# An untied rotary product and a re-searched order in a two-layer attention trunk

## The chip, the cores and the metric

One core of a Trainium2 chip runs the whole program. The metric is the device time of one execution in microseconds. Every time below comes from the runs of the kernel before or from one profiled execution of it.

## The reference

The program computes a decoder trunk of two layers on one sequence of 256 tokens of width 1024. Each layer projects the normalised stream, runs attention with 16 heads of 64, gates it, projects it back, and adds a gated per-layer embedding. Layer 0 is block attention (with 256 tokens it is plain causal attention within one block), layer 1 has a compressed, a selected-block and a windowed branch. What the change touches is the norm and rotation of queries and keys:

```python
def rms_norm(x, gain):
    y = xf * lax.rsqrt(jnp.mean(xf * xf, axis=-1, keepdims=True) + NORM_EPS)
    return (y * gain)
def rope(x, pos):
    ...
    x1, x2 = xf[..., :half], xf[..., half:]
    return jnp.concatenate([x1 * cos - x2 * sin, x2 * cos + x1 * sin], axis=-1)
def moba_layer(h, w_in, q_gain, k_gain, w_out, pos):
    q, k, v, z = jnp.split(h @ w_in, 4, axis=-1)
    q = rope(rms_norm(split_heads(q, N_HEADS), q_gain), pos)
    k = rope(rms_norm(split_heads(k, N_HEADS), k_gain), pos)
    v = split_heads(v, N_HEADS)
    o = merge_heads(moba_attention(q, k, v)) * jax.nn.silu(z)
    return o @ w_out
def reference(...):
    for i in range(DEPTH):
        h = rms_norm(x, norm_gain[i])
        x = x + (moba_layer if i % 2 == 0 else nsa_layer)(h, ...)
        gate = jax.nn.sigmoid(rms_norm(x, ple_gate_gain[i]) @ ple_w_gate[i])
        x = x + gate * (p[i] @ ple_w_proj[i])
```

## The kernel before

**The work.** All weights pass through the core once, in tiles of 128x1024 f32 (512 KB) that SyncE's queue loads into five `raw` buffers. A float32 product is made of reduced-precision parts: ScalarE copies a tile to its rounded part `hi`, VectorE subtracts to get `lo` (`lo<-raw,hi`), and TensorE runs three products (high by high, high by low, low by high) into PSUM banks `mm`. Activations are split in the same way (`a`, `hl`). Scores go into banks `s`, are masked and scaled by VectorE (`sm<-s,...,nr_q`, which also gives the row's extreme in `nb`), exponentiated by ScalarE, divided by their sums `l` (`sm<-sm,l`, on VectorE or ScalarE), and transposed by TensorE (`tr<-cst,sm`).

**The rotation.** `rope()` takes 512 columns of queries or keys, 8 heads of 64, for two halves of 128 tokens. ScalarE squares them, VectorE sums the squares per head (`ssq`) and makes `r0` by two small `tensor_scalar`s, GpSimd raises `r0` to the power -1/2 (`r_q`, `r_k`), and for queries VectorE negates that into `nr_q`, which scales the scores. The rotation itself is two products with a sine table (`turn(t, 0)` and `turn(t, 1)`: `tmp<-q,tq`), one product with a cosine table (`q<-q,tq`) and a sum (`q<-q,tmp`) for each half; `finish()` issues what does not stand ahead of the power. In most rotations the factors are read from the bank of the matmul (`mm`). For the second eight heads of layer 0 (steps `1q` and `1k` of the order) the steps `1qe` and `1ke` have ScalarE copy the bank into the tile `q` or `k` first (`rope_evac`), so that both factors of each product lie in SBUF.

**The order.** Nothing is issued as it is written. Each operation is recorded, and `Plan.schedule`, a greedy list scheduler with a table of costs, places them on the engines; all are then emitted from one line, L400 of the profile. Ties go to what was recorded first, so the sequence of step names in the string `PROGRAM` sets the priorities. Names there are units of projections (`1q.2`), loads (`w:...`), head pairs (`S` scores, `T` transposes, `V` values), evacuations, and so on; names that begin with `n` or a group number are layer 1's. `nc.together(since)` glues the operations recorded since then into one run on their engine, with nothing between them: in `rope()` these are the two `r0` operations and `turn(0, 0)`. The profile names tiles by what the buffer is called first: `r` stands for `r0`, `hl` for the split pair of queries and keys of a head pair, `tq` and `tk` for the tables. Some evacuations may go to either ScalarE or VectorE, by what the scheduler finds free.

**The end.** The last stage is the gate of layer 1: eight units of matmuls (`ng0a` to `ng1b`), each evacuated by a chain (ScalarE copies half a bank, VectorE adds the other half and multiplies by `bc`, ScalarE takes a tanh, VectorE multiplies by the embedding and adds to `xT`), and the output is stored.

Of the kernel before, what the change touches and what calls it, by code (L numbers as in the profile page):

```python
# [24 lines left out]

PROGRAM = ("x0 w:c0 c0 x1 w:c1 c1 x2 w:c2 x3 w:c3 x4 w:c4 w:k.0 x5 c2 w:c5 c3 x7 consts tq a.1 x6 a.3 a.5 a.6 w:c6 a.7 w:c7 "
# [24 lines left out]

STORES = 5

# [368 lines left out]
def trunk(ctx: ExitStack, tc: tile.TileContext, a, out):  # L422
# [14 lines left out]
    def tmp(name):  # L437
        return work.tile([P, 512], F32, tag="tmp", name=name, bufs=5)
# [37 lines left out]
    def tables(name, gain, gains):  # L476
        t = work.tile([P, 2, 2, len(gains), HD], F32, tag=name[:2] + str(len(gains)), name=name, bufs=1)
        for b, g in enumerate(gains):
            for i, c in enumerate((cos, sin)):
                nc.vector.tensor_tensor(t[:, i, :, b], c, gain[:, g, i][:, None].to_broadcast([P, 2, HD]), op=OP.mult)  # L480
        return t
# [186 lines left out]
        return o  # L668

    def rope(ps, tab, nb, norm, is_q, tag, bufs, o=None):  # L670
        if o is None:
            o = work.tile([P, 2, 512], F32, tag=tag, name=tag, bufs=bufs)
        else:
            ps = [o[:, t] for t in range(2)]
        o = o.rearrange("p t (h d) -> p t h d", d=HD)
        ssq = work.tile([P, 2, 8], F32, tag="ssq", name="ssq")
        for t in range(2):
            sq = tmp("hsq").rearrange("p (h d) -> p h d", d=HD)
            nc.scalar.activation(sq.rearrange("p h d -> p (h d)"), ps[t], AF.Square)
            nc.vector.tensor_reduce(ssq[:, t], sq, axis=AX.X, op=OP.add)  # L680
        r0 = work.tile([P, 2, 8], F32, tag="r0", name="r0")
        g = 8 // nb
        qss = [tmp("qs").rearrange("p (b g d) -> p b g d", b=nb, d=HD) for _ in range(2)]
        vs = [ps[t].rearrange("p (b g d) -> p b g d", b=nb, d=HD) for t in range(2)]

        def tb(i, t, lo, hi):
            return tab[:, i, t, :, None, lo:hi].to_broadcast([P, nb, g, hi - lo])

        def turn(t, c):
            lo, hi = 32 * c, 32 * c + 32  # L690
            nc.vector.tensor_tensor(qss[t][:, :, :, lo:hi], vs[t][:, :, :, 32 - lo:64 - lo], tb(1, t, lo, hi), op=OP.mult)

        since = len(nc.ops)
        for t in range(2):
            nc.vector.tensor_scalar(r0[:, t], ssq[:, t], 1.0 if is_q else 1.0 / HD,
                                    norm.e2[:, 0 if is_q else 1, t:t + 1], op0=OP.mult, op1=OP.add)

        turn(0, 0)
        nc.together(since)
        r = work.tile([P, 2, 8], F32, tag="r_" + tag, name="r_" + tag, bufs=bufs)  # L700
        nc.gpsimd.tensor_tensor(r.rearrange("p t h -> p (t h)"), r0.rearrange("p t h -> p (t h)"), neg_half, op=OP.pow)
        if is_q:
            nr = work.tile([P, 2, 8], F32, tag="nr_" + tag, name="nr_" + tag, bufs=bufs)
            nc.vector.tensor_scalar(nr, r, -1.0, None, op0=OP.mult)
        def finish():
            for t in range(2):
                ot = o[:, t].rearrange("p (b g) d -> p b g d", b=nb)
                if t:
                    turn(t, 0)
                turn(t, 1)  # L710
                nc.vector.tensor_tensor(ot, vs[t], tb(0, t, 0, HD), op=OP.mult)
                nc.vector.tensor_tensor(ot, ot, qss[t], op=OP.add)
                if not is_q:
                    nc.vector.tensor_tensor(o[:, t], o[:, t], r[:, t, :, None].to_broadcast([P, 8, HD]), op=OP.mult)

        return o, (nr if is_q else None), finish
# [227 lines left out]
    class Half:  # L944
# [17 lines left out]
        def q(self):  # L962
            self.Q, self.nr, self.q2 = rope(self.u["q"].ps, tab["q"], 1, n0, True, "q", 2, self.early.get("q"))

        def k(self):
            self.K, _, self.k2 = rope(self.u["k"].ps, tab["k"], 1, n0, False, "k", 2, self.early.get("k"))
# [126 lines left out]
    def tabs2():  # L1093
# [4 lines left out]
                ntk=lambda: tab1.update(k=tables("tk1", gnsa, [2, 3])))  # L1098
# [163 lines left out]
    def rope_k():  # L1262
        ST["kk"], _, todo["KE+"] = rope(units["ks"].ps, tab1["k"], 2, n2, False, "q", 2)
# [55 lines left out]
    def KD(i):  # L1319
        w = ST["wins"][:, 960 * i:960 * i + 960].rearrange("p (t g n) -> p t g n", t=16, g=4)  # L1320
        cg = ST["cc"][i].rearrange("p (g t) -> p g t", g=4)
        for h in range(2):
            src = cg[:, :, 16 * h:16 * h + 240].rearrange("p g (n t u) -> p t g n u", t=8, u=2)[:, :, :, :, 0]
            nc.vector.tensor_tensor(w[:, 8 * h:8 * h + 8], src,
                                    pe[:, i, 8 * h:8 * h + 8, None, None].to_broadcast([P, 8, 4, 15]), op=OP.add)
        ST["win"][i] = w.rearrange("p t g n -> p t (g n)")
# [77 lines left out]
    for g in range(4):  # L1404
# [3 lines left out]
                KD0=lambda: KD(0), KD1=lambda: KD(1))  # L1408
# [134 lines left out]
```

## Time and profile before

| | us |
|---|---|
| median of 3 runs | 359.84 |
| lowest and highest run | 358.97, 360.23 |
| profiled execution, its own time | 358.39 |
| its span in the profile | 356.6 |
| TensorE busy in it | 349.5 (98%) |
| VectorE busy | 333.1 (93%) |
| ScalarE busy | 277.1 (78%) |
| GpSimd busy | 32.9 (9%) |

The profiled execution is 1.45 us (0.4%) shorter than the median of the runs and shorter than each of them; 1.79 us of its time lie outside the span. Its mean granted clock of TensorE is 0.998. The shares are averages over the span: what bounds a stage is read from the windows of that stage and from what each engine waited for there.

### The profile page before, as it was taken

To read this page: it belongs to the slowest core of one execution; us is meant where nothing else is said; L and a number is where in the kernel's file an instruction comes from. 1 tells how busy PE (TensorE), PEld (TensorE's weight loads), DVE (VectorE), ACT (ScalarE), POOL (GpSimd) and SP (SyncE) were. 2 spreads that over 40 slices of the span, in tenths; PEclk is the share of its full clock that TensorE was granted. 3 is DMA by queue.
4 is the path that set the end of the run, shared out by engine and by line. 5 is a ranking of instruction groups with operands and counts; after the bars stand their busy time and mean duration, and the time that the engine had idled before them with its cause. 6 is when DMAs were issued, how large, how long until landed. Compare 5 with 4: busy or idle time off the path is not lost.

```text
span 356.6 us, 6708 instructions
## 1 busy us (share of the span) xinstructions
PE 349.5 (98%) x2311; PEld 307.1 (86%) x2311; DVE 333.1 (93%) x846; ACT 277.1 (78%) x622; POOL 32.9 (9%) x26
## 2 busy tenths in 40 slices
PE   8999999989999999999999999999999999999995
PEld 7888888867999888888889999877998998888884
DVE  5899999979999999989999999999999999899875
ACT  5785699957999946768674899988989999857532
POOL 1044200432000000000003300003020000000000
PEclk9999999999999999999999999999999999999999
DMA  8989562711715367474636754427672331266012
GB/s 270 354 325 278 210 227 78 249 59 37 259 63 176 96 205 237 125 234 144 207 99 190 211 172 153 139 84 287 219 239 90 119 120 59 65 199 211 0 47 74
DMA packets 20770, 58.95 MB, mean 165 GB/s; under 512 B 2560, under 2 KB 6016, under 8 KB 20736
## 3 DMA queue, kind: packets, MB, share of 16 engines
q1 hardware_dynamic: 20160, 58.04, 50.2%
q10 hardware_dynamic: 576, 0.48, 0.4%
q8 instruction: 18, 0.29, 0.4%
q14 instruction: 16, 0.13, 0.1%
HBM read 57.46 MB, written 1.05 MB: 164 GB/s over the span
## 4 chain that ended last, share of the span: by engine, by line
PE 95%; DVE 2%; POOL 2%; ACT 0%; issue 0%; DVEq 0%; ACTq 0%
PE mm L400 75%; PE tr L400 13%; PE s L400 6%; POOL r_q L400 2%; DVE lo L400 1%; DVE sm L400 0%; DVE q L400 0%; DVE ssq L400 0%; DVE tmp L400 0%; DVE hl L400 0%; ACT hl L400 0%; DVE r L400 0%; ACT tmp L400 0%; DVE xT L400 0%; DVEq L1538 0%
## 5 line engine op out<-in xcount | busy, mean ns | idle before, releaser
L400 PE MATMUL mm<-a,hi 128*128 128x256 f32 (+1 forms) x656 | 153.1, 327 | 0.0
L400 ACT ACTIVATE hi<-raw 128x1024 fp32r<-128x1024 f32 (+2 forms) x100 | 99.8, 1008 | 37.3 <-PE mm L400 21.3
L400 DVE TENSOR_TENSOR lo<-raw,hi 128x1024 fp32r<-128x1024 f32 (+2 forms) x100 | 115.5, 1164 | 6.5 <-ACT hi L400 5.7
L400 PE MATMUL mm<-hi,a 128*128 128x512 f32 (+2 forms) x356 | 103.9, 378 | 0.0
L400 PEld LDWEIGHTS mm<-a,hi 128*128 128x128 f32 x656 | 101.7, 190 | 1.8 <-DVE big L400 0.2
L400 PE MATMUL mm<-a,lo 128*128 128x256 f32 x448 | 103.0, 283 | 0.0
L400 PEld LDWEIGHTS mm<-a,lo 128*128 128x128 f32 x448 | 81.9, 189 | 9.6 <-issue 0.2
L400 PEld LDWEIGHTS mm<-hi,a 128*128 128x128 f32 x356 | 64.6, 192 | 10.4 <-DVE hi L400 0.2
L400 PE MATMUL mm<-lo,a 128*128 128x512 f32 (+2 forms) x178 | 64.1, 375 | 0.0
L400 ACT ACTIVATE sm<-sm,nb 128x128 f32<-128x128 f32 (+1 forms) x96 | 42.8, 451 | 2.5 <-DVE nb L400 2.3
L400 PEld LDWEIGHTS mm<-lo,a 128*128 128x128 f32 x178 | 33.6, 192 | 5.1
L400 DVE CUSTOM_DVE_ANT_0 sm<-s,cst,nr_q 128x256 f32<-128x256 f32 (+1 forms) x80 | 31.7, 428 | 0.3
L400 POOL TENSOR_TENSOR r_q<-r,neg_half 128x16 f32<-128x16 f32 x5 | 18.0, 3593 | 80.9 <-DVE r L400 80.9
L400 ACT ACTIVATE pt<-tr 128x384 f32<-128x384 f32 x48 | 22.3, 489 | 2.1 <-PE tr L400 1.8
L400 PE MATMUL tr<-cst,sm 128*128 128x128 f32 x144 | 23.1, 274 | 0.0
L400 ACT ACTIVATE tmp<-tmp 128x256 f32<-128x256 f32 (+3 forms) x26 | 12.1, 471 | 10.4 <-DVE tmp L400 10.4
L400 PEld LDWEIGHTS tr<-cst,sm 128*128 128x128 f32 x144 | 17.3, 141 | 3.3 <-ACT sm L400 0.8
L400 ACT ACTIVATION_READ_ACCUMULATOR sm<-sm,nb 128x1 f32 x96 | 18.6, 194 | 0.0
L400 POOL TENSOR_TENSOR rstd<-ms,neg_half 128x2 f32<-128x2 f32 x4 | 3.0, 741 | 169.2 <-DVE ms L400 169.2
L400 ACT ACTIVATE a<-xT,gain_in 128x256 fp32r<-128x256 f32 x31 | 14.6, 498 | 4.8 <-DVE xT L400 2.1
L400 DVE TENSOR_TENSOR hl<-tr,hl 64x512 fp32r<-64x512 f32 x24 | 16.5, 689 | 1.2 <-ACT hl L400 0.4
L400 PE MATMUL tr<-pt,v 128*64 128x256 f32 (+1 forms) x192 | 17.1, 330 | 0.0
(170 smaller groups left out, 452.2 us busy)
## 6 DMA issues: line engine op xcount, KB each, us to landing
raw<-in_moba_in SPq DMA_DIRECT2D x28, 512.0 KB, 4.5
raw<-in_nsa_in SPq DMA_DIRECT2D x24, 512.0 KB, 4.2
raw<-in_w_o SPq DMA_DIRECT2D x8, 512.0 KB, 3.7
raw<-in_w_g SPq DMA_DIRECT2D x8, 512.0 KB, 4.3
raw<-in_w SPq DMA_DIRECT2D x8, 512.0 KB, 4.0
raw<-in_w_no SPq DMA_DIRECT2D x8, 512.0 KB, 3.6
raw<-in_w_ng SPq DMA_DIRECT2D x8, 512.0 KB, 4.1
raw<-in_ple_proj SPq DMA_DIRECT2D x4, 512.0 KB, 4.8
```

The lines of the kernel that those rows point to most:

```text
L400: getattr(getattr(self.nc, o.engine), o.method)(*[real(x) for x in o.args], **{k: real(x) for k, x in o.kwargs.items()})
```

## The change

Two things. First, in `rope()` the product `turn(0, 0)` is recorded ahead of the power, and glued behind the `r0` operations, only where the factors are read from the matmul's bank. For copied queries and keys it is recorded in `finish()`, free to be placed anywhere. Second, the string `PROGRAM` is another one from the masks of layer 0 on, through both layers to the end. The scheduler, its costs, the buffers and all sizes are the same.

```diff
@@ PROGRAM (about 30 lines of it, of which the first changed one)
-           "w:1q.0 w:1q.3 1q.0 masks w:1k.0 consts1 A0 w:1q.1 w:1k.2 w:1k.3 A2 S2 w:1q.2 S0 v A3 1q.1 S3 w:1v.0 w:1v.1 "
...
+           "w:1q.0 w:1q.3 1q.0 masks w:1k.0 A0 w:1v.0 w:1q.1 A3 w:1v.1 w:1q.2 w:1v.2 S3 1q.1 1q.2 1q.3 w:1k.2 S0 A2 1k.0 1qe "
...
@@ rope()
-        if o is None:
+        in_bank = o is None
+        if in_bank:
             o = work.tile([P, 2, 512], F32, tag=tag, name=tag, bufs=bufs)
...
-        turn(0, 0)
+        if in_bank:
+            turn(0, 0)
         nc.together(since)
...
         def finish():
             for t in range(2):
...
-                if t:
+                if t or not in_bank:
                     turn(t, 0)
                 turn(t, 1)
```

What the two do to VectorE's queue at the copied queries' rotation, between the two `r_0<-ssq` operations and the `hl` operations that follow. Names are the buffers' (`q_139` the copied queries, `tq_0_129` their tables, `s_154` and `s_155` score banks, `r_q_145` GpSimd's power, `tr_75` a bank of transposed queries and keys). VectorE before:

```order
L400 TENSOR_SCALAR r_0_142<-ssq_140,e_0_135 128x8 x2
L400 TENSOR_TENSOR tmp_82<-q_139,tq_0_129 128x8x32
L400 TENSOR_TENSOR tmp_83<-q_139,tq_0_129 128x8x32
L400 TENSOR_TENSOR tmp_82<-q_139,tq_0_129 128x8x32
L400 TENSOR_TENSOR tmp_83<-q_139,tq_0_129 128x8x32
L400 TENSOR_TENSOR lo_123<-raw_126,hi_115 128x1024
L400 TENSOR_TENSOR q_139<-q_139,tq_0_129 128x512 x2
L400 TENSOR_SCALAR nr_q_147<-r_q_145 128x16
L400 TENSOR_TENSOR q_139<-q_139,tmp_82 128x512
L400 TENSOR_TENSOR q_139<-q_139,tmp_83 128x512
L400 TENSOR_TENSOR hl_150<-tr_75,hl_150 64x512 x2
```

Behind the two `r_0` stand seven operations on two SBUF tiles each, then `nr_q`, the sums and `hl`. VectorE after, the same place, in two pieces:

```order
L400 TENSOR_SCALAR r_0_142<-ssq_140,e_0_135 128x8 x2
L400 ISA sm_68,nb_156<-s_154,tmp_85,nr_q_146 128x128
L400 ISA nb_156 128x1
L400 TENSOR_TENSOR tmp_86<-s_155,cst_65 128x128
L400 TENSOR_SCALAR sm_71<-sm_71,l_153 128x128
L400 TENSOR_SCALAR sm_71<-sm_71,l_153 128x256
L400 TENSOR_SCALAR sm_72<-sm_72,l_153 128x128
L400 TENSOR_SCALAR sm_72<-sm_72,l_153 128x256
L400 TENSOR_TENSOR tmp_83<-q_139,tq_0_129 128x8x32
L400 TENSOR_TENSOR tmp_84<-q_139,tq_0_129 128x8x32
L400 ISA sm_71,nb_157<-s_155,tmp_86,nr_q_146 128x128
L400 ISA nb_157 128x1
```

```order
L400 ISA sm_71,nb_157<-s_155,cst_65,nr_q_146 128x256
L400 ISA nb_157 128x1
L400 TENSOR_TENSOR tmp_83<-q_139,tq_0_129 128x8x32
L400 TENSOR_TENSOR tmp_84<-q_139,tq_0_129 128x8x32
L400 TENSOR_TENSOR q_139<-q_139,tq_0_129 128x512
L400 TENSOR_SCALAR nr_q_147<-r_q_145 128x16
L400 RECIPROCAL l_152<-l_152 128x4
L400 TENSOR_TENSOR q_139<-q_139,tmp_83 128x512
L400 TENSOR_TENSOR a_113<-tmp_82,a_113 128x256
L400 TENSOR_TENSOR q_139<-q_139,tq_0_129 128x512
L400 TENSOR_TENSOR lo_123<-raw_124,hi_115 128x1024
L400 TENSOR_TENSOR q_139<-q_139,tmp_84 128x512
```

The products now stand behind operations on score banks and four `sm<-sm,l`, and in two pairs; `nr_q` has the cosine product of one half ahead of it, and behind it come the sums, the other half's product and the split `lo_123` that was ahead of it before; the two `hl` operations are the next row. Ahead of the `r_0` operations VectorE has ten `sm` and small operations and one split less than it had before (they come later), and one table product more. On TensorE, ahead of the first matmul that reads these `hl`, some 0.2 us of small matmuls more stand in the queue. For the copied keys, the power in the new order likewise has two `sm<-sm,l`, operations on banks and over twenty more rows between the `r` operations and its first reader.

At the other end, VectorE's queue in the gate of layer 1, where the last weight tiles are split. Each unit there is `tmp<-tmp,mm` (a bank's half added), `tmp<-tmp,bc`, `SCALAR_TENSOR_TENSOR tmp<-tmp,big` and `xT<-xT,tmp`. Before:

```order
L400 TENSOR_SCALAR ms_132<-tr_75 128x2
L400 TENSOR_SCALAR e_1_136<-ms_132 128x2 x2
L400 TENSOR_TENSOR lo_120<-raw_126,hi_118 128x1024
L400 TENSOR_TENSOR tmp_85<-tmp_85,mm_79 128x256
L400 TENSOR_TENSOR lo_122<-raw_127,hi_117 128x1024
L400 TENSOR_TENSOR tmp_85<-tmp_85,bc_137 128x256
L400 SCALAR_TENSOR_TENSOR tmp_86<-tmp_86,big_88 128x256
L400 TENSOR_TENSOR tmp_82<-tmp_82,mm_80 128x256
L400 TENSOR_TENSOR xT_63<-xT_63,tmp_86 128x256
L400 TENSOR_TENSOR tmp_82<-tmp_82,bc_137 128x256
L400 SCALAR_TENSOR_TENSOR tmp_83<-tmp_83,big_88 128x256
```

After:

```order
L400 TENSOR_TENSOR tmp_86<-tmp_86,mm_80 128x256
L400 TENSOR_TENSOR tmp_86<-tmp_86,bc_137 128x256
L400 SCALAR_TENSOR_TENSOR tmp_85<-tmp_85,big_88 128x256
L400 TENSOR_TENSOR tmp_82<-tmp_82,mm_78 128x256
L400 TENSOR_TENSOR xT_63<-xT_63,tmp_85 128x256
L400 TENSOR_TENSOR tmp_82<-tmp_82,bc_137 128x256
L400 SCALAR_TENSOR_TENSOR tmp_84<-tmp_84,big_88 128x256
L400 TENSOR_TENSOR tmp_83<-tmp_83,mm_81 128x256
L400 TENSOR_TENSOR xT_63<-xT_63,tmp_84 128x256
L400 TENSOR_TENSOR tmp_83<-tmp_83,bc_137 128x256
L400 TENSOR_TENSOR lo_123<-raw_128,hi_116 128x1024
L400 SCALAR_TENSOR_TENSOR tmp_86<-tmp_86,big_88 128x256
```

Before, the last split (`lo_122`) stands ahead of the first unit's product with `bc`; after, two splits stand in the two rows ahead of this piece, and a last one (`lo_123`) stands behind the third unit's product with `bc`. TensorE has 13.7 us of matmuls behind the transposes of the last norm where it had 13.2, by the matmuls' steps before.

In numbers: TensorE has the same matmuls, and its queue is the same up to the work of about 45 us. VectorE has eight more `sm<-sm,l` in layer 1 (70 for 62), ScalarE eight fewer; one `hl` copy and one cast go from VectorE to ScalarE. GpSimd's queue has the same order. SyncE's queue has the same 141 rows, the first 44 in the same order; from there the load of `p` stands two rows earlier, and the constants of layer 1 and the embedding's projection weights later.

44 rows, old and new, of the table PROGRAM are left out of this document.

## The prediction

> **What bounds the kernel now.** I read the page's busy shares first, then busy time by stretches of 10 us, then what TensorE waited for, then the chain of waits that ended last, and last the instructions around the one gap that these views agree on. The windows' columns are the stretch and its length, then busy time (and number) on PE, PEld, DVE, ACT and POOL, then the granted clock, the DMA share and GB/s; the lines behind them are TensorE's waits, as us in total, times, longest.
>
> ```profile
> PE 349.5 (98%) x2311; PEld 307.1 (86%) x2311; DVE 333.1 (93%) x846; ACT 277.1 (78%) x622; POOL 32.9 (9%) x26
> 60.00:70.00 10.00, 10.00 (x57) 8.37 (x56) 10.00 (x22) 9.95 (x24) 2.98 (x1) 1.00 0.65 211
> 70.00:80.00 10.00, 8.23 (x49) 6.84 (x48) 7.08 (x22) 6.26 (x11) 4.24 (x2) 1.00 0.21 75
> 80.00:90.00 10.00, 10.00 (x76) 7.92 (x76) 9.97 (x24) 8.10 (x18) 2.14 (x1) 1.00 0.19 58
> 350.00:356.60 6.60, 2.34 (x20) 2.14 (x18) 3.43 (x12) 1.26 (x4) 0.00 (x0) 0.87 0.26 80
> PE s L400 <- ACT hl L400: 1.8, 1, 1.8
> PE tr L400 <- DVE ones L400: 1.1, 1, 1.1
> ```
>
> TensorE is the bound: 349.5 of 356.6 us, at clock 1.00, full in the windows on both sides of 70 to 80. That window alone lacks 1.77 us, and the list names the wait: a score matmul that reads `hl`. The other wait, 1.1 us, is of the start, and 4.26 us lie in the last window: with them the 7.1 us that TensorE is not busy (356.6 - 349.5) are told. So an order can gain about 2 us in the middle and hardly more. The chain shows what the gap hangs on (start, length, engine, tile), and the timeline below it the same stretch (start, length, instruction, in brackets the idle time before it):
>
> ```profile
> 66.58 0.37 DVE r L400 x2
> 67.02 6.37 POOL r_q L400
> 73.50 1.29 DVE q L400 x2
> 74.81 0.69 DVE hl L400
> 75.53 0.42 ACT hl L400
> 76.00 0.62 PE s L400 x3
> 76.62 0.23 PE mm L400
> ```
> ```profile
> 66.57 0.38 DVE L400 TENSOR_SCALAR r<-ssq,e 128x8 f32<-128x8 f32 x2
> 66.84 1.44 DVE L400 TENSOR_TENSOR tmp<-q,tq 128x256 f32<-128x256 f32 x4
> 67.02 6.36 POOL L400 TENSOR_TENSOR r_q<-r,neg_half 128x16 f32<-128x16 f32 x1 [29.50 <-DVE r L400]
> 68.18 1.23 DVE L400 TENSOR_TENSOR lo<-raw,hi 128x1024 fp32r<-128x1024 f32 x1
> 69.31 1.30 DVE L400 TENSOR_TENSOR q<-q,tq 128x512 f32<-128x512 f32 x2
> 73.41 0.17 DVE L400 TENSOR_SCALAR nr_q<-r_q 128x16 f32<-128x16 f32 x1 [2.79 <-POOL r_q L400]
> 73.84 0.39 PE L400 MATMUL mm<-hi,a 128*128 128x512 f32 x1
> 75.53 0.41 ACT L400 ACTIVATE hl<-hl 64x256 fp32r<-64x256 f32 x1 [2.62 <-DVE hl L400]
> 76.00 0.62 PE L400 MATMUL s<-hl 128*128 128x256 f32 x3 [1.77 <-ACT hl L400]
> 76.26 0.42 ACT L400 ACTIVATE hl<-hl 64x256 fp32r<-64x256 f32 x1 [0.31 <-DVE hl L400]
> ```
>
> VectorE comes to `nr_q` at 70.61 (69.31 + 1.30), waits 2.79 us for GpSimd's power, and everything behind `nr_q` in its queue moves with it: the two sums of `q`, and the two `hl` splits, which do not read the power at all. ScalarE then waits 2.62 us and TensorE 1.77.
>
> Why does this power take 6.36 us? Others of the same shape, and VectorE's work around one of them:
>
> ```profile
> 23.16 2.90 POOL L400 TENSOR_TENSOR r_q<-r,neg_half 128x16 f32<-128x16 f32 x1 [2.63 <-DVE r L400]
> 188.70 2.90 POOL L400 TENSOR_TENSOR r_q<-r,neg_half 128x16 f32<-128x16 f32 x1 [0.88 <-DVE r L400]
> 22.98 0.42 DVE L400 TENSOR_TENSOR tmp<-mm,tq 128x256 f32<-128x256 f32 x1
> 23.31 2.35 DVE L400 TENSOR_TENSOR lo<-raw,hi 128x1024 fp32r<-128x1024 f32 x2
> ```
>
> 2.90 us is the free price, so this one was held for 3.46. What VectorE ran from 66.84 to 70.61 are seven operations, each with two tiles in SBUF (`q` is a copy, not the matmul's bank), and 67.02 + 6.36 - 2.90 = 70.48 is where that train ends. At 23.16 the operation at the power's start read `mm`, a bank; two splits with two SBUF tiles began 0.15 us later and took 2.35 us, and the power still needed 2.90. So what holds a power is a two-tile train that is running when it wants to begin, not one that comes later. The Trainium skill ("SBUF — State Buffer", Who interferes with whom) says that VectorE with two SBUF inputs and GpSimd reading SBUF exclude each other through a shared port pair. The held power agrees with it. Its further rule, that the first to issue holds the other for a whole instruction, is weighed among the rivals.
>
> **The change part by part.** *The untied product.* In the copied queries' and keys' rotation the first product is no longer glued behind the two `r` operations; it is counted the same, 0.34 us a piece (four start at 66.84, the next instruction at 68.18), only elsewhere: cost 0. What follows `r` decides the power's start. The new order puts there an `sm<-s` of a bank, a `tmp<-s` of a bank and four `sm<-sm,l`, then products, two more `sm<-s`, products. The prices of these forms (busy us, mean ns of one):
>
> ```profile
> L400 DVE CUSTOM_DVE_ANT_0 sm<-s,cst,nr_q 128x256 f32<-128x256 f32 x48 | 22.2, 481 | 0.0
> L400 DVE CUSTOM_DVE_ANT_0 sm<-s,tmp,nr_q 128x128 f32<-128x128 f32 x16 | 5.4, 348 | 0.1
> L400 DVE TENSOR_SCALAR sm<-sm,l 128x256 f32<-128x256 f32 x35 | 11.7, 354 | 0.1
> L400 DVE TENSOR_SCALAR sm<-sm,l 128x128 f32<-128x128 f32 x27 | 7.4, 285 | 0.1
> L400 DVE TENSOR_TENSOR tmp<-s,cst 128x128 f32<-128x128 f32 x16 | 4.5, 287 | 0.4 <-PE s L400 0.3
> L400 DVE TENSOR_TENSOR lo<-raw,hi 128x1024 fp32r<-128x1024 f32 x88 | 106.9, 1224 | 6.3 <-ACT hi L400 5.7
> ```
>
> VectorE's instructions overlap by some 0.08 us (the split at 68.18 lasts 1.23, the next starts at 69.31), so each counts 0.08 less. From `r` to `nr_q`: two small `sm<-s` 0.54, one wide 0.40, `tmp<-s` 0.21, `sm<-sm,l` 2 x 0.205 + 2 x 0.275 = 0.96, four products 1.34, one `q<-q,tq` 0.60: 4.05 us. The power starts 0.07 us after `r` (66.95 to 67.02 in before), beside an operation that reads a bank, and ends 2.97 us after it. So `nr_q` finds it ready by 1.1 us. If the four `sm<-sm,l` held it, it would start 1.44 us after `r` (0.27 + 0.21 + 0.96) and `nr_q` would wait 0.3. I take no hold: the nearest row is that of 23.16.
>
> Where does that put `hl`? Ahead of `r` the new order leaves out of VectorE's queue (they come later) three `sm<-s` with their `tmp` and `l` (1.24 us), five `sm<-sm,l` (1.17) and one split (1.14), and has one small table product more (about 0.3): `r` ends 3.2 us earlier, at 63.7. From `nr_q` (67.8) to the first `hl` stand its own 0.1, two sums and one product of `q` at 0.6, a split 1.14, a reciprocal and a 128x256 product (0.1 + 0.34): first `hl` at 71.3, ScalarE's two copies out at 72.4 and 73.2 (by the steps from 74.81 to 75.94 and 76.68). TensorE was ready at 76.00 - 1.77 = 74.23; the new order gives it 0.2 us more work ahead (two small matmuls), so 74.4. Even the second copy is 1.2 us ahead of that; the wait goes whole. Its size is 1.77 by the list, and 1.93 by start to start (73.84 to 76.00 is 2.16 us for a matmul that takes 0.23, as at 76.62): **-1.9 us**, with bounds 0 (held as before) and -2.2 (all of that window's excess). For the keys' power (2.90 to 3.00 us, never waited for in before) the new order leaves over twenty rows before its reader: 0.
>
> *The new order beyond.* TensorE has the same matmuls, and up to some 45 us the same order: 0. GpSimd's queue keeps its order. On SP's queue the first 44 rows are the same, then the loads of `p` come a little earlier and the constants of layer 1 later; the DMA share is 0.19 to 0.82 in the six inner windows shown here, and the weights are loaded up to five buffers ahead: 0, as long as that lead holds. VectorE takes eight `sm<-sm,l` from ScalarE in layer 1 (4 x 0.205 + 4 x 0.275 = 1.9 us) and gives back an `hl` copy and a cast: +1.1 us in all. ScalarE, 78% busy, is relieved.
>
> What covers this is the scores' stage of layer 1, and the cover is thin:
>
> ```profile
> 210.00:220.00 10.00, 10.00 (x80) 9.65 (x79) 9.85 (x30) 8.89 (x24) 0.00 (x0) 1.00 0.46 141
> 240.00:250.00 10.00, 10.00 (x92) 6.95 (x91) 9.15 (x35) 7.83 (x22) 3.16 (x2) 1.00 0.82 297
> 290.00:300.00 10.00, 10.00 (x89) 8.81 (x88) 9.85 (x42) 9.95 (x34) 0.00 (x0) 1.00 0.26 86
> ```
>
> From the first to the last `sm<-s` of this layer VectorE's work, each instruction at its form's median step, is 83.7 us before and 86.9 after; TensorE's work between the last `sm<-s` and the last transpose's place (TensorE's sum ahead of the one less VectorE's ahead of the other) falls from 10.4 to 9.2 us. So VectorE's lead shrinks by 1.2 us at the end of the scores. Against that it regains 2.79 in the seventies where TensorE regains 1.9: 0.9 of lead. What is late next is a transpose of `sm`, by 1.2 - 0.9 = **+0.3 us**; the bounds are 0 (before had spare lead there) and +3.2 (all the added work of the stage on TensorE's path).
>
> *The tail.* The end is a chain of TensorE, then ScalarE and VectorE in turn:
>
> ```profile
> 340.96 0.42 DVE L400 SCALAR_TENSOR_TENSOR tmp<-tmp,big 128x256 f32<-128x256 f32 x1 [0.48 <-ACT tmp L400]
> 342.94 0.43 DVE L400 SCALAR_TENSOR_TENSOR tmp<-tmp,big 128x256 f32<-128x256 f32 x1 [0.54 <-ACT tmp L400]
> 352.38 0.49 DVE L400 TENSOR_TENSOR tmp<-mm,bc 128x128 f32<-128x128 f32 x2
> ```
>
> One gate unit costs 1.98 us (340.96 to 342.94), of which VectorE idles 0.54. After the change a last split stands inside this chain: 1.14 - 0.54 = +0.6; but TensorE has 13.7 us of work behind the norm's last transposes where it had 13.2, so the chain begins 0.5 us earlier against the end. I take 0, with bounds -0.3 and +0.6.
>
> Sum: -1.9 + 0.3 + 0 = -1.6 us. The profiled execution took 358.39 us, 1.45 below the median of the runs (359.84) and below each of them; its span would become 355.0 and its time 356.8. Taken from the median, 358.2.
>
> **The rivals.** *The power is freed, but it blocks VectorE instead.* By an exclusive lock the power, first at 63.8, would stop the first two-tile or in-place operation behind it, and VectorE would stand from 0.48 us after `r` for 2.5 us. Then `hl` comes at 73.8, its first copy at 74.9, and TensorE waits about 0.6 in place of 1.9: 359.84 - 1.3 + 0.3 = 358.8, just within what cannot be told. Against it: the splits of 23.31 ran at full speed under a power. The Trainium skill ("SBUF — State Buffer", Who interferes with whom) is for it: the first to issue has the pair for its whole instruction, and `tensor_scalar` too can take it in a two-port mode. By that page the sum would be this rival's; the row at 23.31 is against it. Put in with it, that the change does not do what it says: the power is held after all through every operation to `nr_q`; then 4.05 + 2.90 us pass, and the gain is nil, 360.1. Together 0.08.
>
> *The wait goes, the order gives it back.* VectorE is 9.2 to 10 us busy per 10, so small lateness of a transpose or a split becomes a TensorE wait at once. A giveback of 0.8 to 3.0 us in many pieces is no change: around 359.5. For: the shrunken lead of 1.2 us, and a whole order newly made from 45 us on. Against: before, with the same density, TensorE's list of waits holds nothing behind 80 us. 0.21.
>
> *VectorE becomes the bound in layer 1's scores.* If its lead there is already used up when the stage begins, the added 3.2 us falls whole on TensorE: 359.84 - 1.9 + 3.2 = 361.1, slower. It decides from 3.0 us of new waits on. For: 9.85 of 10 busy at 210 and 290. Against: 0.85 us idle at 240, and TensorE without a gap throughout, so some lead there is. 0.14.
>
> **How the numbers follow.** The likeliest, 0.57: the wait gone, 0 to 0.8 us given back, 357.5 to 358.7. A measurement of this kernel tells 0.3% (1.08 us) from no change, that is below 358.76 or above 360.92. The first and second rival lie inside that: 0.29; the third above: 0.14. The range for 8 in 10 goes from 357.0 (the whole -2.2 and the runs' spread of 0.6 below it) to 360.6 (2.7 us of givebacks): some 0.05 is left below it, 0.12 above.
>
> **What would show it.** Right: the 70 to 80 window has TensorE full, the power of the copied queries takes 2.90 us and starts at about 63.8, `nr_q` has no wait for GpSimd, no matmul `s<-hl` waits there. In the tail the last split lies between two gate units. Wrong, by the first rival: a 2.9 us power with a VectorE operation beside it that is stretched or starts late. By the second: several TensorE waits of 0.1 to 0.5 us for `sm` or `lo`. By the third: TensorE windows between 205 and 305 below 9.7, with waits for `sm` and VectorE at 10.00. A load that lands late (`hi` waiting for DMA behind 50 us, which the sum puts at 0) would also make it wrong.

## The result and the profile after

The changed kernel takes 356.64 us (median of 14 runs, 355.73 to 358.52); the kernel before, run beside it, 358.39 us (14 runs, 357.96 to 360.23). The ratio is 0.9943, with a 95% interval of 0.9928 to 0.9959: faster by 0.57%, or 1.75 us between the medians (2.03 us between the means, 358.69 and 356.66, whose ratio that is). The forecast was 1.6 us of gain and 358.2 us; the gain came out near, the time lies 0.4 us under the range. A ratio leaves out a run that is more than 1.5% above the fastest of its kernel; in all of the runs below that is one, of 361.71 us.

The page's busy line, the three windows around the old gap, and TensorE's list of waits, all of the kernel after:

```profile
PE 348.7 (98%) x2311; PEld 306.1 (86%) x2311; DVE 334.5 (94%) x852; ACT 275.7 (78%) x616; POOL 28.1 (8%) x26
60.00:70.00 10.00, 10.00 (x56) 8.42 (x55) 9.88 (x37) 9.76 (x27) 2.90 (x1) 1.00 0.34 118
70.00:80.00 10.00, 10.00 (x63) 8.97 (x62) 9.88 (x25) 9.59 (x23) 3.13 (x1) 1.00 0.30 107
80.00:90.00 10.00, 10.00 (x85) 8.58 (x85) 9.91 (x21) 8.16 (x17) 0.00 (x0) 1.00 0.30 104
PE tr L400 <- DVE ones L400: 1.1, 1, 1.1
PE mm L400 <- DVE hi L400: 0.8, 1, 0.8
PE mm L400 <- ACT hi L400: 0.3, 1, 0.3
```

The window of 70 to 80 went from 8.23 to 10.00, and the wait for `hl` is gone from the list. What is left is of the start (all before 20 us). The stretch itself, after:

```profile
64.08 0.35 DVE L400 TENSOR_SCALAR r<-ssq,e 128x8 f32<-128x8 f32 x2
64.34 0.34 DVE L400 CUSTOM_DVE_ANT_0 sm<-s,tmp,nr_q 128x128 f32<-128x128 f32 x1
64.51 2.90 POOL L400 TENSOR_TENSOR r_q<-r,neg_half 128x16 f32<-128x16 f32 x1 [26.39 <-DVE r L400]
64.82 1.00 DVE L400 TENSOR_SCALAR sm<-sm,l 128x128 f32<-128x128 f32 x4
65.73 0.75 DVE L400 TENSOR_TENSOR tmp<-q,tq 128x256 f32<-128x256 f32 x2
68.35 0.17 DVE L400 TENSOR_SCALAR nr_q<-r_q 128x16 f32<-128x16 f32 x1
72.09 1.41 DVE L400 TENSOR_TENSOR hl<-tr,hl 64x512 fp32r<-64x512 f32 x2
75.11 0.87 PE L400 MATMUL s<-hl 128*128 128x256 f32 x6
```

The power takes 2.90 us in place of 6.36, `nr_q` finds it ready 0.94 us early (67.41 to 68.35), and no bracket stands behind the last row: TensorE did not wait. VectorE's four `sm<-sm,l` and the products ran at their usual length beside the power.

### The profile page after: what moved, and what is told of

It is laid out like the page before. It is cut to its first block, busy times and chain, and to the rows that moved or that the text cites. A ratio compares the mean times of both kernels' runs of the same rounds, so it can differ in the third digit from the quotient of the medians.

```text
span 355.1 us, 6704 instructions
## 1 busy us (share of the span) xinstructions
PE 348.7 (98%) x2311; PEld 306.1 (86%) x2311; DVE 334.5 (94%) x852; ACT 275.7 (78%) x616; POOL 28.1 (8%) x26
## 4 chain that ended last, share of the span: by engine, by line
PE 94%; DMA 3%; SPq 1%; ACT 1%; DVE 0%; ACTq 0%; issue 0%; DVEq 0%
PE mm L400 76%; PE tr L400 13%; PE s L400 6%; DMA xT<-in_x 2%; DMA tmp<-in_wq 1%; SPq L400 1%; ACTq L400 0%; ACT tmp L400 0%; DVE tmp L400 0%; ACT hi L400 0%; ACT a L400 0%; DVE xT L400 0%; DVEq L1540 0%
## 5 line engine op out<-in xcount | busy, mean ns | idle before, releaser
L400 PE MATMUL mm<-a,lo 128*128 128x256 f32 x448 | 104.1, 284 | 0.0
L400 DVE CUSTOM_DVE_ANT_0 sm<-s,cst,nr_q 128x128 f32<-128x128 f32 (+1 forms) x80 | 32.1, 423 | 0.9 <-PE s L400 0.8
L400 POOL TENSOR_TENSOR r_q<-r,neg_half 128x16 f32<-128x16 f32 x5 | 14.5, 2901 | 76.0 <-DVE r L400 76.0
L400 DVE TENSOR_SCALAR sm<-sm,l 128x128 f32<-128x128 f32 (+1 forms) x70 | 18.8, 316 | 0.1
```

The costliest lines, as they stand in the source:

```text
L400: getattr(getattr(self.nc, o.engine), o.method)(*[real(x) for x in o.args], **{k: real(x) for k, x in o.kwargs.items()})
```

## The experiments

Two kinds are used. Some let the scheduler place everything anew. The others take the order that the scheduler made, of before or of after, and move or add single instructions on one engine (`move` puts them behind a given one; `V` is VectorE's order, `r0` the place of the last `r` operation in it), so that nothing else changes. Each diff below shows the one line that does it; the helpers around it are left out.

**The `hl` splits ahead of `nr_q`, in the order of before.**

```diff
+    order = move(order, [V[r0 + k] for k in (8, 9, 10)], V[r0 + 12])   # nr_q and the two sums behind hl
```

> The order of before, except that VectorE does the two hl splits ahead of nr_q and the two sums of q instead of behind them; the tie and everything else stay. Theory A (the wait is one of place in VectorE's queue: the splits need no power, they only stand behind the operation that does): the power stays held at 6.3 to 6.4 us, nr_q still waits for it, about 1.4 us less long than 2.8, and the matmul s<-hl no longer waits; 1.9 us less than before, ratio 0.995. Rival B (the gain of the change comes from the new order in many places): no change, ratio 1.000. Rival C (the rest of the queue behind nr_q is as urgent as hl, so the wait only moves): a TensorE wait of 1 to 1.8 us a little later, ratio 0.998 to 1.000.

Measured: 357.36 us, ratio 0.9955 (0.9939 to 0.9971).

```profile
67.53 6.36 POOL L400 TENSOR_TENSOR r_q<-r,neg_half 128x16 f32<-128x16 f32 x1 [29.38 <-DVE r L400]
71.16 1.41 DVE L400 TENSOR_TENSOR hl<-tr,hl 64x512 fp32r<-64x512 f32 x2
73.92 0.17 DVE L400 TENSOR_SCALAR nr_q<-r_q 128x16 f32<-128x16 f32 x1 [1.36 <-POOL r_q L400]
75.61 0.90 PE L400 MATMUL tr<-cst,sm 128*128 128x128 f32 x5 [0.29 <-DVE sm L400]
```

The power is held as long as ever, `nr_q` waits for it, and most of the gain is there all the same. What TensorE paid for was the place of `hl` in VectorE's queue, not the power. A piece of rival C is true: 0.29 us of wait came back one step later, at the transposes of `sm`, whose divisions stood behind the sums.

**One more instruction behind `r`, in the order of before.**

```diff
+    order.insert(order.index(V[r0]) + 1, V[r0 - 3])   # the second ssq reduce once more
```

> The order of before with one instruction added: the second ssq reduce (0.68 us, one SBUF input) is done a second time on VectorE, directly behind the two r operations, where the two-tile train began. Theory A (a power is held only by a two-tile or two-port operation that runs when it reads its input, some 0.13 us after its start): the power takes 2.90 us, nr_q comes 0.6 us later in VectorE's queue and finds it ready, no TensorE wait at 76; 1.9 us less than before in spite of 0.6 us more VectorE work, ratio 0.995. Rival D (any two-tile operation during the 2.9 us holds it, or is held by it): the power takes over 5 us or VectorE stands for some 2 us, and the time is that of before or up to 0.6 us more, ratio 1.000 to 1.002.

Measured: 356.39 us, ratio 0.9935 (0.9913 to 0.9957).

```profile
66.74 0.35 DVE L400 TENSOR_SCALAR r<-ssq,e 128x8 f32<-128x8 f32 x2
67.13 0.69 DVE L400 TENSOR_REDUCE ssq<-tmp 128x8 f32<-128x512 f32 x1
67.17 2.90 POOL L400 TENSOR_TENSOR r_q<-r,neg_half 128x16 f32<-128x16 f32 x1 [29.37 <-DVE r L400]
67.73 1.42 DVE L400 TENSOR_TENSOR tmp<-q,tq 128x256 f32<-128x256 f32 x4
71.41 0.16 DVE L400 TENSOR_SCALAR nr_q<-r_q 128x16 f32<-128x16 f32 x1
```

A useless 0.69 us on a 93% busy engine buys as much as the whole change. The reduce has one SBUF input and runs when the power begins; the two-tile train that begins 0.56 us later neither holds the power (2.90) nor is held by it (four products in 1.42 us, 1.44 before). TensorE's queue is that of before, matmul for matmul, so the two traces can be laid over each other from an early matmul on: the lead over before is 1.93 us at the old wait, 2.15 us some 1.1 us behind it, and 2.19 us at the last matmul. The gain is made at this one place, and nothing of it needs the new order in the other 280 us.

**Only the untying, and only the new string of steps.** The first takes the rope() part of the diff alone, the second the string alone.

> Only the first half of the change: the product is untied in before, the string of steps stays the old one. The scheduler then puts that product ahead of r, and one of the two hl splits ahead of nr_q; the train behind r is still two-tile operations. Theory A: the power is still held, 6.0 us, but half of what TensorE waits for comes out early; the wait of 1.77 falls to 0 to 0.5, ratio 0.995 to 0.997. Rival B (many places): no change, ratio 0.999 to 1.001. If the untying itself freed the power: 2.9 us and no wait for it by nr_q.

> Only the second half: the new string of steps, with the product tied behind r as in before. Theory A: the power starts beside one product of 0.42 us and is held for 0.2 to 0.3 us, then VectorE reads banks; 3.1 to 3.2 us, nr_q does not wait, no TensorE wait; the time of the whole change, ratio 0.994. Rival E (the untying is what brings the gain): the power is held by several us and the ratio is 0.999 or more.

Measured: the untying alone 359.95 us, ratio 1.0028 (1.0011 to 1.0044); the string alone 378.43 us, ratio 1.0551 (1.0520 to 1.0582). First, lines of the untying alone, its last row the window of 120 to 130:

```profile
67.45 6.02 POOL L400 TENSOR_TENSOR r_q<-r,neg_half 128x16 f32<-128x16 f32 x1 [29.82 <-DVE r L400]
70.74 0.68 DVE L400 TENSOR_TENSOR hl<-tr,hl 64x512 fp32r<-64x512 f32 x1
74.31 0.69 DVE L400 TENSOR_TENSOR hl<-tr,hl 64x512 fp32r<-64x512 f32 x1
76.10 0.62 PE L400 MATMUL s<-hl 128*128 128x256 f32 x3 [1.09 <-DVE hl L400]
120.00:130.00 10.00, 9.38 (x65) 6.77 (x66) 10.00 (x23) 5.58 (x17) 0.00 (x0) 1.00 0.29 79
```

The power was held for 3.12 us (6.02 - 2.90), as expected, and the second `hl` stood behind `nr_q`: the wait fell to 1.09, not to the 0 to 0.5 expected. Then the scheduler's other decisions, all different behind this place, lost more than that between 119 and 127 us with VectorE at 10.00. Lines of the string alone:

```profile
L400 POOL TENSOR_TENSOR r_q<-r,neg_half x5: 2901/2902/3007, 23.1 to 256.5; 128x16 f32<-128x16 f32 x5
200.00:210.00 10.00, 5.91 (x46) 5.47 (x45) 9.86 (x19) 8.67 (x14) 2.90 (x1) 0.93 0.57 184
210.00:220.00 10.00, 7.44 (x34) 6.46 (x35) 8.04 (x23) 6.35 (x16) 0.00 (x0) 0.56 0.16 52
PE tr L400 <- DVE k_1r L400: 4.1, 1, 4.1
```

Here the local part of the theory holds (no power of this kind is held by more than 0.11 us: 3007 ns at most), and the expected time was quite wrong: one tie fewer or more sends the greedy scheduler down another path, and the string fits only the code that it was searched with. Layer 1's split keys (`k_1r`) come 4 us late for TensorE. Both numbers say nothing on what the tie costs; for that it must be put into the same order.

**The tie in the order of after.** Only the product that the tie would hold is moved.

```diff
+    order = move(order, [V[r0 + 7]], V[r0])   # the first tmp<-q,tq directly behind r
```

> The changed kernel's order with the first product tmp<-q,tq alone moved back to directly behind the two r operations, where the tie would hold it; nothing else moves. It runs from 0.08 us ahead of r's end for 0.42 us, so it runs when the power reads. Theory A: the power takes 3.1 to 3.2 us, nr_q does not wait, four sm<-sm,l come 0.34 us later: the time of the changed kernel within what can be told, ratio to before 0.994 to 0.996. If the untying itself carries the gain in this order: the power is held by more than 1 us and the ratio is 0.998 or more.

Measured: 356.73 us, ratio 0.9939 (0.9919 to 0.9960).

```profile
64.26 3.01 POOL L400 TENSOR_TENSOR r_q<-r,neg_half 128x16 f32<-128x16 f32 x1 [26.11 <-DVE r L400]
```

One tied product holds the power for 0.11 us, and the time is that of the change. In this order the untying by itself is worth nothing that can be measured.

**A train put back behind `r`, in the order of after.**

```diff
+    order = move(order, [V[r0 + k] for k in (7, 8, 11, 12, 13)], V[r0])   # four tmp<-q,tq, one q<-q,tq
```

> The changed kernel with a two-tile train put back behind r: all four products tmp<-q,tq and one q<-q,tq stand directly behind the two r operations, ahead of the score operations; nr_q keeps its row. Theory A: the power is held until the train ends, 4.6 to 4.7 us in place of 2.90; nr_q, asked for 3.9 us after r, waits about 0.8, the hl splits come 0.8 later, and TensorE, which needs them 2 us later still, does not wait: the time of the changed kernel, ratio to before 0.994. Rival F (a held power costs by itself): the 0.8 us show in the time, ratio 0.996 or more. Rival G (the product at the head is the only thing that holds a power): 3.1 us.

Measured: 358.11 us, ratio 0.9969 (0.9950 to 0.9988).

```profile
64.17 4.61 POOL L400 TENSOR_TENSOR r_q<-r,neg_half 128x16 f32<-128x16 f32 x1 [26.39 <-DVE r L400]
66.75 0.81 PE L400 MATMUL tr<-cst,sm 128*128 128x128 f32 x4 [1.17 <-DVE sm L400]
68.81 0.17 DVE L400 TENSOR_SCALAR nr_q<-r_q 128x16 f32<-128x16 f32 x1 [0.73 <-POOL r_q L400]
```

The hold and `nr_q`'s wait are as forecast (4.61, 0.73), and no score matmul waits for `hl`. The time is 1 us worse for a reason that the expectation left out: the train pushed the four `sm<-sm,l` back by nearly 2 us, and TensorE waited 1.17 us for them at 66.75. By its time alone this run would have spoken for rival F; the list of waits shows that it does not.

**Four `tensor_scalar`s behind `r`, in the order of after.**

```diff
+    order = move(order, [V[r0 + k] for k in (3, 4, 5, 6)], V[r0])   # four sm<-sm,l
```

> The changed kernel with its four tensor_scalar sm<-sm,l (one SBUF tile in and out, 1.0 us together) moved directly behind the two r operations, so that they run when the power reads its input. If a tensor_scalar takes the shared ports as a two-tile operation does: the power is held until the four are done, 3.6 to 3.7 us. If only two-tile operations hold it: 2.90. In either case nr_q, asked for 3.9 us after r, hardly waits, and the time is that of the changed kernel, ratio to before 0.993 to 0.995.

Measured: 356.99 us, ratio 0.9930 (0.9907 to 0.9952).

```profile
64.12 1.00 DVE L400 TENSOR_SCALAR sm<-sm,l 128x128 f32<-128x128 f32 x4
64.29 3.13 POOL L400 TENSOR_TENSOR r_q<-r,neg_half 128x16 f32<-128x16 f32 x1 [26.39 <-DVE r L400]
```

Neither expectation: held, but for 0.23 us only, while the four run for 1.00. Here a `tensor_scalar` holds the power, but the row of them lets it in behind the second.

**One `tensor_scalar` between `r` and the two-tile train, in the order of before**, run twice.

```diff
+    order = move(order, [V[r0 - 2]], V[r0])   # sm<-sm,l 128x128
```

> The order of before with one instruction moved: the tensor_scalar sm<-sm,l of 128x128 (0.29 us) that stood ahead of the two r operations stands behind them, ahead of the two-tile train. The power reads at about the moment this instruction ends. If GpSimd gets in when a tensor_scalar ends, as between the four of them (0.23 us of hold there): the power takes 2.9 to 3.1 us, no wait at 76, ratio 0.993 to 0.995. If the next two-tile operation takes over without a gap: 6.2 to 6.4 us, the wait as before, ratio 0.999 to 1.001.

> The kernel with one tensor_scalar between r and the two-tile train once more, for a second profile: its times lay at 355.7 to 356.5 but for one of 358.18, and the one profiled execution showed the power held for the whole train. If the entry between the two is decided anew in each execution: this profile shows 2.9 to 3.1 us and no wait at s<-hl, or 6.5 us and a wait of 1.8, and the times again fall into two groups some 2 us apart, with the profile's own time in the group that fits. If the held power cost nothing here: 6.5 us in a profile whose own time is at 356.

Measured: 356.27 us, ratio 0.9937 (0.9914 to 0.9960), then 356.28 us, 0.9936 (0.9914 to 0.9958). Of the 13 times 11 lie from 355.69 to 356.57; one is 358.18 and one, that of the first profile, 361.71 (it also reached its first power of this kind, elsewhere at 22.8 to 24.3 us, at 25.0). The two profiles, first and second:

```profile
68.75 0.29 DVE L400 TENSOR_SCALAR sm<-sm,l 128x128 f32<-128x128 f32 x1
68.93 6.55 POOL L400 TENSOR_TENSOR r_q<-r,neg_half 128x16 f32<-128x16 f32 x1 [29.57 <-DVE r L400]
68.95 1.44 DVE L400 TENSOR_TENSOR tmp<-q,tq 128x256 f32<-128x256 f32 x4
78.11 0.63 PE L400 MATMUL s<-hl 128*128 128x256 f32 x3 [1.78 <-ACT hl L400]
```
```profile
66.41 0.28 DVE L400 TENSOR_SCALAR sm<-sm,l 128x128 f32<-128x128 f32 x1
66.58 3.21 POOL L400 TENSOR_TENSOR r_q<-r,neg_half 128x16 f32<-128x16 f32 x1 [29.40 <-DVE r L400]
66.61 1.45 DVE L400 TENSOR_TENSOR tmp<-q,tq 128x256 f32<-128x256 f32 x4
```

The same queue, with the same steps to within 0.01 us up to the power's start, gives a long hold in one execution and one of 0.31 us in the other. In both the first two-tile product begins 0.02 to 0.03 us after the power. In the second the power got in when that product ended (at 67.03), with six two-tile operations still behind it; in the first only when all seven had ended. What decides between the two is not shown. With the power held, the old wait of 1.78 us is back, in the old order, and with nothing glued to `r`.

**The power three times, in the order of after.**

```diff
+    k = order.index(power)
+    order[k:k] = [power, power]
```

> The changed kernel with the power of the copied queries done three times in a row on GpSimd (the same inputs and output), so that its result comes 5.8 us later. Theory A: nr_q waits 4.8 to 4.9 us, the first hl moves from 72.1 to 76.9, TensorE waits 2.9 to 3.1 us at s<-hl (its slack of about 2 us used up): 0.994 + 0.008 = 1.002 to 1.003 of before. If what stands behind nr_q were not on TensorE's path: no change against the changed kernel, 0.994. If the lateness passed on whole, without slack: 4.9 us, 1.008.

Measured: 362.44 us, ratio 1.0077 (1.0050 to 1.0104).

```profile
73.89 0.18 DVE L400 TENSOR_SCALAR nr_q<-r_q 128x16 f32<-128x16 f32 x1 [5.15 <-POOL r_q L400]
78.62 0.62 PE L400 MATMUL s<-hl 128*128 128x256 f32 x3 [3.04 <-ACT hl L400]
79.71 0.62 PE L400 MATMUL s<-hl 128*128 128x256 f32 x3 [0.47 <-ACT hl L400]
80.00:90.00 10.00, 9.61 (x58) 8.62 (x59) 9.59 (x33) 7.49 (x18) 3.13 (x1) 0.83 0.29 105
```

The wait at `s<-hl` is what the chain from power to TensorE gives (3.04, expected 2.9 to 3.1), so the chain and its 2 us of slack are right. But the kernel lost 4.8 us against the change (1.0077 - 0.9943 of 359), not 3; in the profiled execution, the longest of its four, TensorE took 6.0 us more from matmul number 150 to the last. Of the rest, 0.47 and 0.39 us are waits behind it, and the last row shows what had not been reckoned with: the granted clock is 0.83 over the next 10 us (1.7 us of TensorE's work), after a gap in TensorE's work.

**New steps for layer 0, then the old ones.** The untied product, with the string's steps up to `z0>1` in their new order and all others in their old.

> The untied product with the new string of steps up to the end of layer 0's z projection, and from there the steps in their old order. Theory A (all of the gain is the wait at 76): 0.993 to 0.996, as the changed kernel. Rival B (the new order behind that place carries some of the gain, or the two do not fit together): 0.998 or more, with TensorE waits behind 130 us.

Measured: 362.83 us, ratio 1.0082 (1.0054 to 1.0109).

```profile
PE mm L400 <- DVE tmp L400: 3.9, 2, 3.3
170.00:180.00 10.00, 8.54 (x26) 6.76 (x27) 6.21 (x14) 3.81 (x9) 0.00 (x0) 0.66 0.35 104
```

The power is free here (2.90 us), and the seam between two orders costs more than it gains: a wait of 3.3 us from 168 on, and again a clock of 0.66 over the 10 us from 170. As with the first pair, half of a searched order is no experiment on the other half.

**The change once more**, beside the tie and the one `tensor_scalar`.

> The changed kernel itself once more, beside the two above. Ratio to before 0.993 to 0.996; whether TensorE reaches its 150th instruction at 34.97 us again, or at 34.2 as in the one profile of before, tells whether the start-up differs by chance or by the change: by chance is expected, since the queues are the same there.

Measured: 356.52 us, ratio 0.9935 (0.9914 to 0.9955); its span is 354.5. TensorE's matmul number 150 (counted from 0) starts at 34.22 us, in the first profile of after at 34.97, in that of before at 34.21, in the others from 33.97 to 36.31: the start-up differs by chance. So before (356.6) and this execution (354.5) are the fair pair of spans: 2.1 us.

## Why the prediction was right, and where it was wrong

**The wait (-1.9): right.** Each step came out: `r` ended 0.7 us later than forecast (64.43 for 63.7), of which the later start-up of this execution explains 0.6 to 0.76; the power was free; VectorE took 3.92 us from `r` to `nr_q` (4.05 forecast); `hl` began at 72.09 (71.3, or 72.0 by this start-up); no wait. In the second profile of the change, whose start-up is that of before, `r` ended at 63.67 and `hl` began at 71.33, as forecast. The second copy of `hl` was ready 0.5 us ahead of TensorE (74.59 to 75.11), less than the 1.2 claimed. That the place of `hl` behind `nr_q` was the price is shown by the run with `hl` first, and that the train behind `r` was the cause by the extra reduce. Two readings were loose: no row gives the bound of -2.2 as the window's excess, which is 1.77, and the split at 68.18 overlaps the next operation by 0.10 us, not 0.08. The sum of -1.6 hardly hangs on either.

**The givebacks (+0.3): none.** From the start of TensorE's matmul number 150 to that of its last one 317.85 us passed before and 315.61 after, 2.24 less. That is the wait of 1.93 and 0.3 more, and the extra reduce, which leaves TensorE's queue as it was, has nearly the same (2.19): there 0.2 came within 1.1 us behind the wait. So the new order elsewhere gained and lost next to nothing in sum. No transpose of `sm` waited in layer 1, though VectorE has 1.4 us more to do (334.5 for 333.1). The lead that was said to shrink by 1.2 us was enough for that; the term should have been nought. That the sum of -1.6 lies so near the 1.75 between the medians is partly luck, since the traces differ by 2.1 to 2.2 us.

**The tail (0): right.** From the start of the last matmul to the end 4.55 us before and 4.54 after. The split among the gate units lengthened one unit by 0.5 us, and the last unit still waited only for its matmul.

**The base: wrong, and the range with it.** The step that failed is "taken from the median, 358.2". The median of three, 359.84, was taken as the kernel's time and the profiled 358.39 as a low draw. Of 58 runs of before, made beside the experiments, 41 have a mean granted clock of 0.997 or more and a median of 358.51; the other 17, at 0.994 to 0.995, have 360.08 and none lies under 359.25. The times of 359.84 and 360.23 among the first three lie where that second group lies, though two of the 41 reach 360.1 and 360.4 as well and the clocks of the three are not known; the profiled execution, with 0.998, belonged to the first. Against the profiled execution the prediction itself gives 356.8, with 356.64 measured. And the range's lower end allowed 0.6 us for the spread of the runs, where the base alone was 1.45 us too high (359.84 for 358.39).

**The rivals.** The lock on VectorE did not show: behind a power that had begun, two-tile operations and `tensor_scalar`s ran at their usual length (in the change four `sm<-sm,l` in 1.00 us, with the extra reduce four products in 1.42). A part of it is true: the Trainium skill ("SBUF — State Buffer", Who interferes with whom) counts `tensor_scalar` among the operations that can take the shared ports, and here a row of them held the power for 0.23 us. That the one that comes second waits for the whole instruction of the first is seen for GpSimd behind VectorE, and not for VectorE behind GpSimd. The rivals on the order and on layer 1's scores did not come true in the change; that a new order is a real danger is seen in the three kernels whose scheduling was done anew (0.3 to 5.5% slower).

## What to carry to other kernels

When an engine waits, look at what stands behind the waiting instruction in its queue: work that does not need the late result may simply be put ahead of it, and here that was worth nearly as much as freeing the late result (ratios of 0.9955 and 0.9935). Where a GpSimd instruction is held like this power, try behind the operation that feeds it one VectorE instruction that reads a bank, or a reduce with one SBUF input: with either the power took 2.90 us here, while with a `tensor_scalar` the outcome was open. And before a median of few runs is made the base of a forecast, see whether the profiled execution and the runs agree, and whether the kernel has a gap that may or may not cost it the clock.

## What the runs showed of the hardware

**When a GpSimd instruction is held.** In five profiles the power ended 2.90 us after a point 0.13 to 0.14 us ahead of the end of VectorE's two-tile train (before: 70.48 against 70.61; with `hl` first 70.99 and 71.12; untied only 70.57 and 70.71; train put back 65.88 and 66.02; one `tensor_scalar`, first profile, 72.58 and 72.72). The short holds show the same 0.14 us: with the tie in place 64.37 against the product's end at 64.51, with the four `tensor_scalar`s 64.52 against 64.67, the end of the second. This fits a power that needs its input only for a moment, some 0.14 us after its start; it fits as well records of VectorE that end 0.14 us after the operation has let go, and no run tells the two apart. What is running at that moment holds the power: a single product ahead of a bank operation costs 0.11 us, the row of `tensor_scalar`s 0.23. In a train of two-tile operations the power got in behind the last one in these five profiles, but behind an earlier one in two others: in the second profile with one `tensor_scalar` behind the first of seven (66.89 against 67.03), and the second of the three powers behind a product with `q<-q,tq` next (67.98 against 68.12). A two-tile operation that began 0.15 us or more after the power cost it nothing (the split at 23.31 in before, the train with the extra reduce).

**A gap of 1.8 us may cost twice.** Windows of 2 us in the first profile with one `tensor_scalar`, from the end of its wait, and in before, around the wait of the same length:

```profile
78.00:80.00 2.00, 1.90 (x10) 1.77 (x10) 1.97 (x6) 1.28 (x3) 0.00 (x0) 0.65 0.00 0
80.00:82.00 2.00, 2.00 (x9) 1.71 (x8) 1.97 (x9) 1.60 (x5) 0.76 (x1) 0.50 0.25 68
```
```profile
76.00:78.00 2.00, 2.00 (x14) 1.70 (x15) 1.97 (x6) 1.51 (x3) 0.00 (x0) 1.00 0.00 0
78.00:80.00 2.00, 2.00 (x10) 1.66 (x9) 1.97 (x11) 1.42 (x4) 0.86 (x1) 1.00 0.30 109
```

The same wait is followed by a clock of 0.50 to 0.65 in one execution and of 1.00 in the other. That fits the 17 of 58 runs of before that are 1.57 us slower at a lower mean clock (0.994 to 0.995). None of the 20 runs of the change has one (0.997 to 1.000), nor has any of the 49 runs of the six experiments whose profiles show no gap on TensorE above 1.2 us (`hl` first, extra reduce, untying alone, tie in place, train back, four `tensor_scalar`s). No profile of before caught such an execution, so for before itself it is inferred. The Trainium skill ("TensorE: Matmul & The Clock Gate", What's actually happening) has a window of about 3.4 us that runs freely, and a clock that is halved after at least one such window of idleness. That a gap of half that length may do it differs from the page and rests on this one profile (that of the run of 361.71 us) and on the two groups of times. After gaps of 3.0 us and more (three powers, new then old steps, the string alone) each profile shows a clock of 0.50 to 0.51 over 2 us or more.
